# Stick-breaking attention: the scores copied to SBUF first, and the softplus and its running sum kept in one tile

## The chip, the cores and the metric

The kernel runs on one NeuronCore of a Trainium2 chip. The time is what the device took for one execution, in microseconds (us); lower is better. Five engines run side by side, each with its own queue of instructions, taken in order: TensorE (PE in the profile, with its weight loads as PEld), VectorE (DVE), ScalarE (ACT), GpSimd (POOL) and SyncE (SP), which here issues most transfers. They wait for one another through semaphores. Operands lie in SBUF; a matmul's results lie in PSUM, of which the stage below uses a pool of four banks.

## The reference

One decoder layer over 512 tokens of width 2048 in fp32: a norm, one input projection, two kinds of attention, an output projection, and an MLP of width 8192 with a squared ReLU. The change concerns the second kind, stick-breaking attention, with 16 heads of 64:

```python
z = jnp.einsum('bhqd,bhsd->bhqs', q_blk, kt).astype(jnp.float32) * scale
log_beta = jax.nn.log_sigmoid(z)
log_1m = jnp.where(causal, jax.nn.log_sigmoid(-z), 0.0)
later = lax.cumsum(log_1m, axis=3, reverse=True) - log_1m
w = jnp.where(causal, jnp.exp(log_beta + later), 0.0)
```

The weights w are then multiplied with v. With softplus(z) = max(z,0) + ln(1+exp(-|z|)), masked to the keys before the query, the exponent is z minus the sum of softplus from this key up to the query.

## The kernel before

Every large product is done as three matmuls of a high and a low half (`mm3`, lines 123 to 125). The halves of a weight chunk are made by ScalarE (a cast, line 91) and VectorE (a subtraction, line 92, 128x1024 here).

The stick-breaking heads go in eight pairs (0 to 7). A pair has four blocks of 128 queries (0 to 3); block i sees (i+1)*128 keys, so its tiles are 128 to 512 columns wide. In names such as z_30 and b_31 the first digit is the block and the second the head of the pair. A block has two halves. `begin` issues the score matmuls of both heads into two PSUM banks (line 558, six of them) and then, for each head, this chain:

- ScalarE: absolute value of the scores from PSUM (571), exp (572), ln (573), into tile a
- VectorE: max(z,0)+a into tile b, reading the scores from PSUM (574)
- GpSimd: mask of the diagonal 128x128 of b (575)
- VectorE: running sum of b into a (578), then z minus a into b, reading the scores from PSUM again (580)
- GpSimd: mask of b (581); ScalarE: exp of b, the weights (583)

`end` transposes the weights on TensorE (592, into a PSUM bank named wtr) and VectorE copies them to SBUF (593). After block 3 the pair's product with v follows (609, bank bv).

These blocks are interleaved with the projections' matmuls by `pump`, called after every 12 of them: on odd calls it runs the `begin` of the next block, and three calls after it, once a later block has begun, the matching `end`:

```python
if clock[0] % 2:
    begun = bool(units) and units[0][0] <= clock[0]
    if begun:
        begin, end = units.popleft()[1]
        begin()
        flight.append(end)
    flight.append(None) if not begun and flight else None
elif len(flight) > 1:
    end = flight.popleft()
```

So the transposes of a block stand in TensorE's queue 36 projection matmuls, and the `begin` of the next block, behind its scores. Within what the program says, a scheduler orders each engine's queue by its own estimates, and gives a PSUM bank of the pool of four (scores, wtr and bv together) to the next user of it; a bank is free once its last reader is done.

Of the kernel before, what the change touches and what calls it, by code (L numbers as in the profile page):

```python
# [15 lines left out]
ALU = mybir.AluOpType  # L16
# [4 lines left out]
P = 128  # L21
# [37 lines left out]
def hymba_layer(ctx: ExitStack, tc: tile.TileContext, x, norm_attn_g, w_in, q_norm_g, k_norm_g,  # L59
                sinks, rel_bias, swa_out_g, sb_out_g, w_out, norm_mlp_g, w_up, w_down, sel, eye, out):  # L60
    nc = tc.nc
    x, out = x[0], out[0]
# [23 lines left out]
    def bank(name):  # L86
        return pa.tile([P, 512], F32, tag="pa", name=name)
# [289 lines left out]
    def finish_o(av, branch, c, keep=False):  # L377

        if c == 0:
            nc.scalar.square(out=S[branch], in_=av)  # L380
        else:
            sq = wk.tile([P, T], F32, tag="we", name=f"osq{branch}_{c}")
            nc.scalar.square(out=sq, in_=av)
            nc.gpsimd.tensor_tensor(out=S[branch], in0=S[branch], in1=sq, op=ALU.add)
        if keep:
            return parts(av, branch, c)
        o = wk.tile([P, T], F32, tag="we", name=f"o{branch}_{c}")
        nc.scalar.copy(out=o, in_=av)
        nc.sync.dma_start(out=oscr[8 * branch + c], in_=o)
        return None  # L390
# [158 lines left out]
    def sb_pair(c, q, k, vs, keep):  # L549
        wt, ws_of = [], {}  # L550

        def scores(i):
            wn = max((i + 1) * P, 256)
            sc = [bank(f"z{c}_{i}{s}") for s in range(2)]
            for a, b in ((0, 0), (0, 1), (1, 0)):
                for s in range(2):
                    rows = slice(s * DH, (s + 1) * DH)
                    nc.tensor.matmul(sc[s][:, 0:wn], q[rows, a, i * P:(i + 1) * P], k[rows, b, 0:wn],
                                     start=(a == 0 and b == 0), stop=(a == 1))
            return sc  # L560

        def weights(i, sc):
            w = (i + 1) * P
            dg = slice(i * P, (i + 1) * P)
            ws = []
            for s in range(2):
                z = sc[s][:, 0:w]
                a = wk.tile([P, 512], F32, tag=("wa", "wc")[s], name=f"a{c}_{i}{s}")[:, 0:w]
                b = wk.tile([P, 512], F32, tag=("wb", "wd")[s], name=f"b{c}_{i}{s}")[:, 0:w]

                nc.scalar.activation(out=a, in_=z, func=AF.Abs)
                nc.scalar.activation(out=a, in_=a, func=AF.Exp, scale=-1.0)
                nc.scalar.activation(out=a, in_=a, func=AF.Ln, bias=1.0)
                nc.vector.scalar_tensor_tensor(out=b, in0=z, scalar=0.0, in1=a, op0=ALU.max, op1=ALU.add)
                nc.gpsimd.affine_select(out=b[:, dg], in_=b[:, dg], pattern=[[-1, P]], compare_op=ALU.is_gt,
                                        fill=0.0, base=0, channel_multiplier=1)

                nc.vector.tensor_tensor_scan(out=a[:, ::-1], data0=ones2[:, 0:1].broadcast_to([P, w]),
                                             data1=b[:, ::-1], initial=0.0, op0=ALU.mult, op1=ALU.add)
                nc.vector.tensor_tensor(out=b, in0=z, in1=a, op=ALU.subtract)  # L580
                nc.gpsimd.affine_select(out=b[:, dg], in_=b[:, dg], pattern=[[-1, P]], compare_op=ALU.is_gt,
                                        fill=NEG, base=0, channel_multiplier=1)
                nc.scalar.activation(out=b, in_=b, func=AF.Exp)
                ws.append(b)
            return ws

        def turn(i, ws):
            w = (i + 1) * P
            for s in range(2):
                tr = bank(f"wtr{c}_{i}{s}")  # L590
                for j in range(i + 1):
                    nc.tensor.transpose(tr[:, j * P:(j + 1) * P], ws[s][:, j * P:(j + 1) * P], ident)
                nc.vector.tensor_copy(out=wt[s][:, 0:i + 1, i * P:w],
                                      in_=tr[:, 0:w].rearrange("p (j q) -> p j q", q=P))

        def begin(i):
            ws_of[i] = weights(i, scores(i))

        def end(i):
            if i == 0:  # L600
                wt.extend(wtp.tile([P, 4, 512], F32, tag="wt", name=f"wt{c}_{s}") for s in range(2))
            turn(i, ws_of.pop(i))
            if i < 3:
                return
            av = bank(f"bv{c}")
            cc = c % 4
            for j in range(4):
                for s in range(2):
                    nc.tensor.matmul(av[s * DH:(s + 1) * DH, j * P:],
                                     vs[j][:, (2 * cc + s) * DH:(2 * cc + s + 1) * DH],  # L610
                                     wt[s][:, j, j * P:], start=(j == 0), stop=(j == 3))
            o = finish_o(av, 1, c, keep)
            if o is not None:
                ohl[1, c] = o

        return [(partial(begin, i), partial(end, i)) for i in range(4)]
# [445 lines left out]
    for cj in range(2 * NC):  # L1062
# [8 lines left out]
        for s, (name, ai, _, b, more) in enumerate(d_products(cj)):  # L1071
# [36 lines left out]
            a = act[c, ai]  # L1108
# [45 lines left out]
```

## Time and profile before

| | us |
|---|---|
| median of three runs | 1998.21 (1998.0 to 1998.86) |
| the profiled execution | 1998.97 |
| its span, first to last instruction | 1997.2 |
| TensorE busy | 1976.4 (99%) |
| VectorE busy | 1649.4 (83%) |
| ScalarE busy | 1037.5 (52%) |
| GpSimd busy | 1011.3 (51%) |

The stick-breaking blocks run from 320 to 626 us of the span. A timeline row gives the start, the duration, the engine and line, the tiles written and read with their sizes, how many instructions are merged into the row, and in brackets how long the engine stood idle before it and which instruction ended that. A merged row "x2" of 1.09 us holds two overlapping instructions. The granted clock (PEclk) is TensorE's, 1.00 at 2.4 GHz.

### The profile page before, as it was taken

Reading aid. Unit: us, or ns where it says so; the run is one execution under the profiler, and the core shown is the slowest. Engines: PE = TensorE matmul, PEld = TensorE weight load, DVE = VectorE, ACT = ScalarE, POOL = GpSimd, SP = SyncE. Lnnn points to the kernel's source line nnn. Section 1 sums busy time; section 2 is a strip of 40 time slices with the busy share of each in tenths; the row PEclk is TensorE's granted clock in tenths of the full one; section 3 lists DMA queues with packets and bytes.
Section 4 is the critical chain, followed back from the end, with each engine's and each line's share of the span. In section 5 each row is a group of like instructions: output and inputs, shape, how many; then the busy total and the mean of one; then the engine's idle time right before and its main releaser. Section 6 shows DMA issues by size and latency. Waiting matters only on the chain.

```text
span 1997.2 us, 31358 instructions
## 1 busy us (share of the span) xinstructions
PE 1976.4 (99%) x11652; PEld 1717.5 (86%) x11652; DVE 1649.4 (83%) x2142; ACT 1037.5 (52%) x1900; POOL 1011.3 (51%) x898
## 2 busy tenths in 40 slices
PE   8999999999999999999999999999999999999999
PEld 7887787778777889999999999998888888888887
DVE  4469654664776479999999999999999999999997
ACT  6357544453554575656565656565443333333444
POOL 0013431221321038777777777776866656656653
PEclk9999999999999999999999999999999999999999
DMA  6732332224245555665656565656766457456451
GB/s 224 146 119 80 100 98 83 75 69 137 93 140 172 192 169 180 217 201 189 208 181 215 180 216 181 212 176 245 290 250 250 158 221 291 161 221 261 143 204 67
DMA packets 213916, 350.31 MB, mean 175 GB/s; under 512 B 9779, under 2 KB 154372, under 8 KB 206596
## 3 DMA queue, kind: packets, MB, share of 16 engines
q1 hardware_dynamic: 211216, 345.02, 51.0%
q10 hardware_dynamic: 2548, 3.30, 1.3%
q8 instruction: 91, 1.49, 0.3%
q14 instruction: 61, 0.50, 0.1%
HBM read 270.16 MB, written 78.12 MB: 174 GB/s over the span
## 4 chain that ended last, share of the span: by engine, by line
PE 89%; DVE 5%; ACT 3%; POOL 1%; issue 1%; DMA 1%; POOLq 0%; SPq 0%; DVEq 0%; ACTq 0%
PE ps_u L831 11%; PE ps_u L830 11%; PE ps_u L832 11%; PE ps_d L1119 9%; PE ps_d L1120 9%; PE ps_d L1118 9%; PE ps_qk L123 3%; PE ps_qk L125 3%; PE ps_qk L124 3%; PE ps_o L125 2%; PE ps_o L123 2%; PE ps_o L124 2%; PE ps_qa L123 1%; PE ps_qa L124 1%; PE ps_qa L125 1%; DVE lo_d L92 1%
## 5 line engine op out<-in xcount | busy, mean ns | idle before, releaser
L832 PE MATMUL ps_u<-h2h,lo_u 128*128 128x256 f32 x1792 | 507.5, 283 | 0.1
L830 PE MATMUL ps_u<-h2h,hi_u 128*128 128x256 f32 x1792 | 507.6, 283 | 0.0
L831 PE MATMUL ps_u<-h2l,hi_u 128*128 128x256 f32 x1792 | 507.4, 283 | 0.0
L1118 PE MATMUL ps_d<-hi_d,ad 128*128 128x512 f32 x896 | 348.8, 389 | 2.7 <-ACT e L856 2.7
L1119 PE MATMUL ps_d<-lo_d,ad 128*128 128x512 f32 x896 | 349.0, 390 | 0.1
L1120 PE MATMUL ps_d<-hi_d,ad 128*128 128x512 f32 x896 | 348.7, 389 | 0.0
L832 PEld LDWEIGHTS ps_u<-h2h,lo_u 128*128 128x128 f32 x1792 | 344.1, 192 | 0.3 <-DVE lo_u L92 0.3
L831 PEld LDWEIGHTS ps_u<-h2l,hi_u 128*128 128x128 f32 x1792 | 344.2, 192 | 0.0
L830 PEld LDWEIGHTS ps_u<-h2h,hi_u 128*128 128x128 f32 x1792 | 344.1, 192 | 0.0
L806 POOL TENSOR_TENSOR s_u<-st_u 128x256 f32<-128x256 f32 x256 | 212.1, 849 | 245.1 <-DVE lo_u L92 176.3
L965 POOL TENSOR_TENSOR T<-st_d,T 128x1024 f32<-128x1024 f32 x64 | 174.2, 2724 | 188.3 <-DVE lo_d L92 185.8
L92 DVE TENSOR_TENSOR lo_d<-T,hi_d 128x1024 fp32r<-128x1024 f32 x128 | 250.5, 1971 | 19.5 <-ACT hi_d L91 18.9
L92 DVE TENSOR_TENSOR lo_u<-s_u,hi_u 128x512 fp32r<-128x512 f32 x256 | 261.8, 1023 | 0.3 <-ACT hi_u L91 0.3
L91 ACT CAST hi_u<-st_u 128x384 fp32r<-128x384 f32 x256 | 131.2, 513 | 229.4 <-PE ps_u L831 224.1
L91 ACT CAST hi_d<-T 128x1024 fp32r<-128x1024 f32 x128 | 134.9, 1055 | 188.5 <-PE ps_d L1120 175.6
L92 DVE TENSOR_TENSOR lo_u<-st_u,hi_u 128x384 fp32r<-128x384 f32 x256 | 196.1, 766 | 30.4 <-ACT hi_u L91 29.5
L1118 PEld LDWEIGHTS ps_d<-hi_d,ad 128*128 128x128 f32 x896 | 168.2, 188 | 38.0 <-ACT e L856 3.1
L1119 PEld LDWEIGHTS ps_d<-lo_d,ad 128*128 128x128 f32 x896 | 168.2, 188 | 36.1 <-DVE lo_d L92 1.3
L1120 PEld LDWEIGHTS ps_d<-hi_d,ad 128*128 128x128 f32 x896 | 168.2, 188 | 34.8
L92 DVE TENSOR_TENSOR lo_d<-st_d,hi_d 128x1024 fp32r<-128x1024 f32 x96 | 189.7, 1988 | 9.1 <-ACT hi_d L91 9.0
L91 ACT CAST hi_d<-st_d 128x1024 fp32r<-128x1024 f32 x96 | 101.3, 1056 | 154.3 <-PE ps_d L1120 135.4
L91 ACT CAST hi_u<-s_u 128x512 fp32r<-128x512 f32 x256 | 158.5, 619 | 18.0 <-POOL s_u L806 18.0
(242 smaller groups left out, 3818.9 us busy)
## 6 DMA issues: line engine op xcount, KB each, us to landing
st_u<-in_w_up SPq DMA_DIRECT2D x128, 512.0 KB, 3.7
st_d<-in_w_down SPq DMA_DIRECT2D x64, 1024.0 KB, 8.3
ad<-ac SPq DMA_DIRECT2D x56, 1024.0 KB, 6.3
ac<-ah SPq DMA_DIRECT2D x32, 896.0 KB, 4.0
ac<-al SPq DMA_DIRECT2D x32, 896.0 KB, 5.8
st_qk<-in_w_in SPq DMA_DIRECT2D x64, 256.0 KB, 3.0
st_o<-in_w_out SPq DMA_DIRECT2D x32, 512.0 KB, 4.2
st_qa<-in_w_in SPq DMA_DIRECT2D x16, 512.0 KB, 4.0
```

Of the source, the lines that this page charges most:

```text
L91: cast = nc.scalar.copy(out=hi, in_=st)
L92: nc.vector.tensor_tensor(out=lo, in0=st, in1=hi.bitcast(F32), op=ALU.subtract)
L123: nc.tensor.matmul(ps, ah, bh, start=first, stop=False)
L124: nc.tensor.matmul(ps, ah, bl, start=False, stop=False)
L806: last_sum[0] = nc.gpsimd.tensor_tensor(out=o, in0=a, in1=b, op=op)
L830: nc.tensor.matmul(o, wh[:, a], hh[:, b], start=first, stop=False, skip_group_check=True)
L831: nc.tensor.matmul(o, wh[:, a], hl[:, b], start=False, stop=False, skip_group_check=True)
L832: nc.tensor.matmul(o, wl[:, a], hh[:, b], start=False, stop=(k == KP - 1), skip_group_check=True)
L965: nc.gpsimd.tensor_tensor(out=o, in0=raw[cj, a, h], in1=raw[cj, b, h], op=ALU.subtract)
L1118: nc.tensor.matmul(o, al, bh[:, kk], start=first, stop=False, skip_group_check=True)
L1119: nc.tensor.matmul(o, al, bl[:, kk], start=False, stop=False, skip_group_check=True)
L1120: nc.tensor.matmul(o, ar, bh[:, kk], start=False, stop=end, skip_group_check=True)
```

## The change

ScalarE first copies the scores of a head from PSUM into b. The sum max(z,0)+a is written over a (it still reads the scores from PSUM), the mask and the running sum work in place on a, and the last subtraction takes b minus a, both in SBUF, in place over b. Tiles, shapes and every other instruction stay. 64 copies are added, one for each head of each block.

```diff
@@ -567,17 +567,18 @@
                 z = sc[s][:, 0:w]
                 a = wk.tile([P, 512], F32, tag=("wa", "wc")[s], name=f"a{c}_{i}{s}")[:, 0:w]
                 b = wk.tile([P, 512], F32, tag=("wb", "wd")[s], name=f"b{c}_{i}{s}")[:, 0:w]
+                nc.scalar.copy(out=b, in_=z)

                 nc.scalar.activation(out=a, in_=z, func=AF.Abs)
                 nc.scalar.activation(out=a, in_=a, func=AF.Exp, scale=-1.0)
                 nc.scalar.activation(out=a, in_=a, func=AF.Ln, bias=1.0)
-                nc.vector.scalar_tensor_tensor(out=b, in0=z, scalar=0.0, in1=a, op0=ALU.max, op1=ALU.add)
-                nc.gpsimd.affine_select(out=b[:, dg], in_=b[:, dg], pattern=[[-1, P]], compare_op=ALU.is_gt,
+                nc.vector.scalar_tensor_tensor(out=a, in0=z, scalar=0.0, in1=a, op0=ALU.max, op1=ALU.add)
+                nc.gpsimd.affine_select(out=a[:, dg], in_=a[:, dg], pattern=[[-1, P]], compare_op=ALU.is_gt,
                                         fill=0.0, base=0, channel_multiplier=1)

                 nc.vector.tensor_tensor_scan(out=a[:, ::-1], data0=ones2[:, 0:1].broadcast_to([P, w]),
-                                             data1=b[:, ::-1], initial=0.0, op0=ALU.mult, op1=ALU.add)
-                nc.vector.tensor_tensor(out=b, in0=z, in1=a, op=ALU.subtract)
+                                             data1=a[:, ::-1], initial=0.0, op0=ALU.mult, op1=ALU.add)
+                nc.vector.tensor_tensor(out=b, in0=b, in1=a, op=ALU.subtract)
                 nc.gpsimd.affine_select(out=b[:, dg], in_=b[:, dg], pattern=[[-1, P]], compare_op=ALU.is_gt,
                                         fill=NEG, base=0, channel_multiplier=1)
                 nc.scalar.activation(out=b, in_=b, func=AF.Exp)
```

From line 570 on the changed kernel's line numbers are one higher than before: the copy is 570, absolute value 572, exp 573, ln 574, max-and-add 575, first mask 576, running sum 579, subtraction 581, second mask 582, the weights' exp 584, transpose 593, its copy 594.

The instructions are also ordered anew. ScalarE, block 3 of pair 1, before, from the last weights of block 2 (b_21) on; hi_qk is a cast for the projections:

```order
L583 ACTIVATE b_21_3616<-b_21_3616 128x384
L571 ACTIVATE a_30_3674<-z_30_3666 128x512
L571 ACTIVATE a_31_3687<-z_31_3667 128x512
L572 ACTIVATE a_30_3674<-a_30_3674 128x512
L572 ACTIVATE a_31_3687<-a_31_3687 128x512
L573 ACTIVATE a_30_3674<-a_30_3674 128x512
L573 ACTIVATE a_31_3687<-a_31_3687 128x512
L91 CAST hi_qk_0_3972<-st_qk_0_3969 128x1024
L583 ACTIVATE b_30_3675<-b_30_3675 128x512
L571 ACTIVATE a_00_3748<-z_00_3740 128x128
L583 ACTIVATE b_31_3688<-b_31_3688 128x512
```

And the same place after the change:

```order
L584 ACTIVATE b_21_3629<-b_21_3629 128x384
L570 COPY b_30_3689<-z_30_3680 128x512
L572 ACTIVATE a_30_3688<-z_30_3680 128x512
L570 COPY b_31_3703<-z_31_3681 128x512
L573 ACTIVATE a_30_3688<-a_30_3688 128x512
L572 ACTIVATE a_31_3702<-z_31_3681 128x512
L574 ACTIVATE a_30_3688<-a_30_3688 128x512
L573 ACTIVATE a_31_3702<-a_31_3702 128x512
L91 CAST hi_qk_0_3994<-st_qk_0_3991 128x1024
L574 ACTIVATE a_31_3702<-a_31_3702 128x512
L584 ACTIVATE b_30_3689<-b_30_3689 128x512
```

Each head now has four instructions ahead of its sum instead of three, the two heads are staggered, and the cast hi_qk stands ahead of the second head's last logarithm. The exps of block 2 stand ahead of block 3's copy as they stood ahead of its absolute value.

VectorE, the same block, before (wt<-wtr are copies of transposes, lo_qk is a subtraction for the projections; the running sum is listed as SCALAR_TENSOR_TENSOR with the tile of ones):

```order
L574 SCALAR_TENSOR_TENSOR b_30_3675<-z_30_3666,a_30_3674 128x512
L574 SCALAR_TENSOR_TENSOR b_31_3688<-z_31_3667,a_31_3687 128x512
L578 SCALAR_TENSOR_TENSOR a_30_3674<-ones_494,b_30_3675 128x512
L578 SCALAR_TENSOR_TENSOR a_31_3687<-ones_494,b_31_3688 128x512
L580 TENSOR_TENSOR b_30_3675<-z_30_3666,a_30_3674 128x512
L580 TENSOR_TENSOR b_31_3688<-z_31_3667,a_31_3687 128x512
L593 COPY wt_0_3568<-wtr_20_3712 128x3x128
L593 COPY wt_1_3569<-wtr_21_3717 128x3x128
L92 TENSOR_TENSOR lo_qk_0_3973<-st_qk_0_3969,hi_qk_0_3972 128x1024
```

And after:

```order
L575 SCALAR_TENSOR_TENSOR a_30_3688<-z_30_3680,a_30_3688 128x512
L594 COPY wt_0_3580<-wtr_20_3728 128x3x128
L579 SCALAR_TENSOR_TENSOR a_30_3688<-ones_494,a_30_3688 128x512
L594 COPY wt_1_3581<-wtr_21_3733 128x3x128
L581 TENSOR_TENSOR b_30_3689<-b_30_3689,a_30_3688 128x512
L575 SCALAR_TENSOR_TENSOR a_31_3702<-z_31_3681,a_31_3702 128x512
L92 TENSOR_TENSOR lo_qk_0_3995<-st_qk_0_3991,hi_qk_0_3994 128x1024
L579 SCALAR_TENSOR_TENSOR a_31_3702<-ones_494,a_31_3702 128x512
L575 SCALAR_TENSOR_TENSOR a_00_3764<-z_00_3756,a_00_3764 128x128
L581 TENSOR_TENSOR b_31_3703<-b_31_3703,a_31_3702 128x512
```

Before, the two heads go side by side and the projections' subtraction comes behind both. Now the first head's chain is finished first, and lo_qk, and the first sum of the next pair's block 0, stand between the steps of the second head.

TensorE, the transposes of block 3 of pair 0 with what they wait for, before:

```order
L592 MATMUL wtr_30_3479<-ident,b_30_3368 128x128 [waits Activation_49]
L592 MATMUL wtr_30_3479<-ident,b_30_3368 128x128 x2
L592 MATMUL wtr_30_3479<-ident,b_30_3368 128x128 [waits Pool_49]
L592 MATMUL wtr_31_3485<-ident,b_31_3381 128x128 [waits Activation_49]
L592 MATMUL wtr_31_3485<-ident,b_31_3381 128x128 x2
L592 MATMUL wtr_31_3485<-ident,b_31_3381 128x128 [waits Pool_49]
```

And after:

```order
L593 MATMUL wtr_30_3489<-ident,b_30_3374 128x128 [waits Activation_49]
L593 MATMUL wtr_30_3489<-ident,b_30_3374 128x128 x2
L593 MATMUL wtr_30_3489<-ident,b_30_3374 128x128 [waits Pool_49]
L123 MATMUL ps_v_3343<-hi_v_2_3516,hT_238 128x512
L124 MATMUL ps_v_3343<-lo_v_2_3517,hT_238 128x512
L125 MATMUL ps_v_3343<-hi_v_2_3516,hT_238 128x512
L123 MATMUL ps_v_3343<-hi_v_2_3516,hT_246 128x512
L124 MATMUL ps_v_3343<-lo_v_2_3517,hT_246 128x512
L125 MATMUL ps_v_3343<-hi_v_2_3516,hT_246 128x512
L593 MATMUL wtr_31_3495<-ident,b_31_3388 128x128 [waits Activation_49]
L593 MATMUL wtr_31_3495<-ident,b_31_3388 128x128 x2
L593 MATMUL wtr_31_3495<-ident,b_31_3388 128x128 [waits Pool_49]
```

The second head's transposes (wtr_31) now come six projection matmuls behind the first head's. The same holds in pairs 3, 4 and 7; in pairs 1, 2, 5 and 6 they stay side by side.

## Rows read from the trace of the kernel before

**Rows 1.** the page, busy time by engine (microseconds, share of the span, instructions)

```profile
PE 1976.4 (99%) x11652; PEld 1717.5 (86%) x11652; DVE 1649.4 (83%) x2142; ACT 1037.5 (52%) x1900; POOL 1011.3 (51%) x898
```

**Rows 2.** waits, 320 to 626 us: engine, line, releaser, total us, times, longest

```profile
DVE b L574 <- ACT a L573: 61.5, 22, 6.0
ACT b L583 <- POOL b L581: 52.9, 28, 3.7
...
PEld z L558 <- DVE b L580: 9.8, 18, 1.1
```

**Rows 3.** windows: engines' busy us, granted clock (1.00 is full), DMA share, GB/s

```profile
core 0: us, PE busy (x) PEld busy (x) DVE busy (x) ACT busy (x) POOL busy (x), PEclk, DMA share, GB/s
343.00:346.00 3.00, 3.00 (x8) 2.20 (x8) 0.96 (x2) 3.00 (x7) 1.28 (x1) 0.56 0.32 59
514.00:517.00 3.00, 1.68 (x9) 0.77 (x7) 3.00 (x7) 0.52 (x1) 1.32 (x3) 1.00 0.00 0
320.00:626.00 306.00, 299.27 (x1449) 226.98 (x1448) 204.95 (x337) 162.74 (x342) 76.95 (x146) 0.99 0.34 105
```

**Rows 4.** timeline, TensorE, pair 1 into 2: start, duration, row, idle before, releaser

```profile
362.18 0.62 PE L558 MATMUL z<-hl_b,hl_b 64*128 64x256 f32 x6
...
376.55 0.50 PE L123 MATMUL ps_v<-hi_v,hT 128*128 128x512 f32 x1
...
382.58 0.39 PE L125 MATMUL ps_v<-hi_v,hT 128*128 128x512 f32 x1
383.61 1.21 PE L558 MATMUL z<-hl_b,hl_b 64*128 64x256 f32 x6 [0.64 <-DVE b L580]
...
387.61 1.04 PE L592 MATMUL wtr<-ident,b 128*128 128x128 f32 x8
```

**Rows 5.** timeline, ScalarE, the same stretch

```profile
375.60 0.99 ACT L583 ACTIVATE b<-b 128x384 f32<-128x384 f32 x2 [2.09 <-POOL b L581]
376.54 1.09 ACT L571 ACTIVATE a<-z 128x512 f32<-128x512 f32 x2
...
384.70 0.62 ACT L583 ACTIVATE b<-b 128x512 f32<-128x512 f32 x1
```

**Rows 6.** timeline, VectorE, the same stretch

```profile
379.21 1.29 DVE L574 SCALAR_TENSOR_TENSOR b<-z,a 128x512 f32<-128x512 f32 x2 [1.80 <-ACT a L573]
380.42 2.56 DVE L578 TENSOR_TENSOR_SCAN a<-ones,b 128x512 f32<-128x512 f32 x2
382.89 1.26 DVE L580 TENSOR_TENSOR b<-z,a 128x512 f32<-128x512 f32 x2
...
385.00 1.21 DVE L92 TENSOR_TENSOR lo_qk<-st_qk,hi_qk 128x1024 fp32r<-128x1024 f32 x1
```

**Rows 7.** timeline, GpSimd, the masks of pairs 0 and 1

```profile
351.16 1.22 POOL L575 TENSOR_SCALAR_AFFINE_SELECT b<-b 128x128 f32<-128x128 f32 x1 [0.24 <-DVE b L574]
...
380.63 1.09 POOL L575 TENSOR_SCALAR_AFFINE_SELECT b<-b 128x128 f32<-128x128 f32 x1 [0.30 <-DVE b L574]
...
384.28 0.29 POOL L581 TENSOR_SCALAR_AFFINE_SELECT b<-b 128x128 f32<-128x128 f32 x1 [0.30 <-DVE b L580]
```

**Rows 8.** groups by shape, 320 to 626 us: count, busy us, mean ns, idle

```profile
L578 DVE TENSOR_TENSOR_SCAN a<-ones,b 128x512 f32<-128x512 f32 x16 | 19.5, 1219 | 1.1 <-POOL b L575 0.4
...
L580 DVE TENSOR_TENSOR b<-z,a 128x512 f32<-128x512 f32 x16 | 10.3, 674 | 0.0
...
L388 ACT COPY o<-bv 128x512 f32<-128x512 f32 x6 | 3.5, 581 | 0.0
```

**Rows 9.** timeline, TensorE, last block of pair 0

```profile
340.68 0.50 PE L558 MATMUL z<-hl_b,hl_b 64*128 64x512 f32 x1 [0.66 <-DVE b L580]
341.94 1.40 PE L558 MATMUL z<-hl_b,hl_b 64*128 64x512 f32 x5 [0.77 <-DVE wt L593]
...
355.56 0.66 PE L592 MATMUL wtr<-ident,b 128*128 128x128 f32 x4 [0.80 <-ACT b L583]
```

**Rows 10.** timeline, TensorE, last block of pair 3

```profile
440.00 1.06 PE L558 MATMUL z<-hl_b,hl_b 64*128 64x512 f32 x6
...
450.01 1.03 PE L592 MATMUL wtr<-ident,b 128*128 128x128 f32 x8
```


## The prediction

> **What bounds the kernel now.** I read the busy times first: TensorE is busy for 99% of the span [rows 1], so only time in which TensorE stands still, or runs at a lower clock, can be gained or lost. Next the windows: the change touches 320 to 626 us, where TensorE is idle for 306.00 - 299.27 = 6.7 us, and some more is lost inside its busy time by a slow clock and by matmuls that start late [rows 3]. Then the waits of that stretch: the release that TensorE's score matmuls wait for is VectorE's subtraction b (line 580), the last reader of the scores, 18 times and 9.8 us on the weight loads [rows 2]. Last the timeline of one place that repeats. When pair 1 ends and pair 2 begins, the scores of pair 2's block 0 start at 383.61, 1.03 us after the projection matmul before them (382.58), where 0.23 is the rhythm: 0.8 lost; and their six matmuls take 1.21 us where the same block shape takes 0.62 without a wait: 0.59 lost [rows 4]. That 1.39 us is there at the end of four pairs (1, 2, 5, 6). Pair 0 loses more: its block 3 scores wait 0.66 and 0.77, its second transposes 0.80 [rows 9], and the clock falls to 0.56 right after [rows 3]. In pair 4 the same two score waits stand within 514 to 517, TensorE 1.68 of 3.00 busy, at a clock of 1.00 [rows 3].
>
> So what ends last is the chain of a block: scores, three ScalarE steps, sum, mask, running sum, subtraction, mask, exp. It holds the scores' banks until the subtraction, and it must end before TensorE wants the weights.
>
> **The change part by part.**
>
> *The earlier release.* The scores' last reader moves from the subtraction (580) to the max-and-add, two VectorE steps sooner. Absolute value and max-and-add still read PSUM, so the copy by itself frees nothing. In pair 1 the banks of pair 2's block 0 then hang on pair 1's first sum and on a copy of block 2's transposes, both due by 383, so the 1.39 us goes: -1.4 in each of four pairs, -5.6. In pair 0 the score waits go too.
>
> *The copies.* No copy of scores is in the trace. The nearest row is ScalarE's copy of a 128x512 PSUM tile, 0.581 us [rows 8]; two absolute values of that size take 1.09, so one more costs about 0.5 of queue [rows 5]. ScalarE is half idle [rows 1], so the two copies cost nothing in throughput; they cost in the chain. By the order, the first head's ln is ScalarE's sixth instruction of the block, not its fifth: +0.5; the second's is eighth behind a cast.
>
> *The subtraction.* From PSUM it takes 0.674 for 512 columns [rows 8]. With both operands in SBUF the nearest row is the projections' subtraction, 1.21 for 1024 [rows 6], so 0.6: no gain worth counting. The Trainium skill, "VectorE: DVE Perf Modes", section "Rules for kernel authors", advises a copy out of PSUM where many operations follow; the rows show 0.674 against 0.6 for the one operation that follows here, so by that page too the sum stays.
>
> *The masks.* A mask of 128x128 on GpSimd takes 0.29 [rows 7]. But it took 1.09 at 380.63, beside the running sum that began at 380.42 [rows 6, 7], and 1.22 at 351.16. It took 0.29 at 384.28 beside the subtraction and copies, which read PSUM [rows 6, 7]. The mask thus waits out a VectorE instruction that began earlier and reads two SBUF tiles. After the change the second mask of the second head comes right behind a subtraction whose follower on VectorE is, in block 2 of pairs 1 and 2, the projections' subtraction (1.21), and in block 3 the next pair's running sum: up to 1.21 - 0.29 = 0.9, and nothing at the least. I take the whole of it, as the row at 351.16 is the same pairing. The Trainium skill, "SBUF — State Buffer", section "Who interferes with whom", says that a VectorE instruction with two SBUF inputs contends with a GpSimd one that reads SBUF, and that the one issued later is blocked; the trace agrees (1.09 against 0.29).
>
> *The new order, pair 1, block 3.* Before: block 2's second exp ends at 376.59, block 3's first sum starts at 379.21 and its second exp ends at 384.70 + 0.62 = 385.32 [rows 5, 6]. The second transposes are wanted half of 1.04 behind the first ones' 387.61 [rows 4], about 388.1, and 386.65 if the 1.39 is gone. After:
> - Block 2: its sum is some 0.35 later by the copies, the two copies of block 1's transposes now stand among its steps (+0.7), and its last mask is locked (+0.9). Its second exp ends at 378.6, not 376.59. It stands ahead of block 3's first copy on ScalarE, so block 3, whose scores are there at 376.55, starts 2.0 late.
> - ScalarE: five instructions of 0.5 and an ln of 0.63 from 378.5: first sum at 381.7.
> - VectorE, in its new order: sum 381.7, copy, running sum 382.85, copy, subtraction 384.45, second head's sum 385.05, projections' subtraction 385.65 to 386.87. That locks the second head's first mask, so its running sum (1.22, rows 8) starts at 387.05; the subtraction starts at 388.43, its mask is locked by the next pair's running sum until 389.5, and the exp ends at 390.1.
> TensorE wants it at 386.65: a wait of 3.45, for 1.39 lost before; with a little on the product with v, +2.3. Without the lock in block 2, as in pairs 5 and 6 where a copy stands between, some 0.65 less. Bounds: with block 2 in time (-2.0) and no lock on the last mask (-0.5) the exp ends at 387.6, a wait of 1.0, net -0.4; with every estimate 1 us late, +3.3.
>
> *Sum.* Pairs 1 and 2: 2 x 2.3. Pairs 5 and 6: 2 x (2.8 - 1.4). Pair 3 loses no time before; its transposes start at 450.01; the second head's, 0.4 behind, move by six matmuls more, so they are wanted at 451.8. Its scores are there at 440.00 + 1.06 = 441.06 [rows 10]; pair 1's chain takes 390.1 - 378.5 = 11.6 from block 2's last exp, which stands here one place later, behind the first absolute value, and costs 0.6: 453.3, so +1.5. Pair 7, the same but with less behind it: +0.2, an estimate. Pair 0 loses its two score waits as starts show them (1.9), the transposes' 0.97 (0.80 of idle and a late start) and the slow clock, (1 - 0.56) x 3.0 = 1.3; it takes a wait like pair 3's: 1.5 - 4.2 = -2.7. Pair 4 gives 3.00 - 1.68 = 1.3 and takes 1.5: +0.2. Together 4.6 + 2.8 + 1.5 + 0.2 - 2.7 + 0.2 = +6.6. Clock: it fell once after waits of 1.4 us and once it did not [rows 3]; of four waits of about 3 us I let two bring a fall at 1.3 each: +2.6. That is +9.2 on the profiled 1998.97, or on the median 1998.21: 2007.4, told as 2007.
>
> **The rivals.**
> - *An even trade.* The scheduled order is not what the engines' own pace gives. If block 2's exp is not late, the new waits are 1.0 to 2 us and eat what the early release gives: between -4 and +4, middle 1998. For it: slack of 1.3 us at block 3 and about 3 us at block 2 in the trace before; against it: the second head's steps stand behind lo_qk by order, not by estimate.
> - *Faster.* One mechanism: the banks. If the last exp of block 3 ends by 386.65 in pair 1's time, no wait comes in place of the released ones. Then 5.6 in four pairs, 4.2 less little in pair 0, and 1.3 in pair 4 go: about -10, 1988. It is decided at the second exp of block 3: 385.32 before, so it may be 1.3 later. For it: every wait of the score matmuls was on the subtraction. Against it: the copies, the order and the locks all push that exp later, 4.8 by the sum above.
> - *Much slower.* The forecast's waits with the clock falling after each of six: 6.6 + 6 x 1.3 = +14.4, 2012; with every chain 1 us later in the six pairs another 6, 2018.
> - *The change does nothing for the banks,* because another reader is last: then the 5.6 and pair 0's 1.9 stay and the chains are late in addition; but the waits for scores delay the wants too, so this is within the forecast's price.
>
> **How the numbers follow.** Forecast 0.55, much slower 0.08, even trade 0.25, faster 0.12. A difference under 0.2% (4 us) can't be told from none here. Faster than 1994: 0.12, from the faster rival. Within 4 us: 0.25. Slower than 2002: 0.63. The range goes from 1995, which takes in nearly all of the even trade, to 2017, short of the last of the much slower case; the forecast's own range is 2003 to 2014.
>
> **What would show it.** After the change no score matmul of a next pair's block 0 waits on VectorE's subtraction; TensorE waits instead on ScalarE's exp at the second transposes of block 3, 3 us or so in pairs 1 and 2, less in 5 and 6, 1 to 2 in pair 3. The masks' mean (second one, 0.3 before) rises. Block 2's second exp ends after block 3's scores are there. VectorE's busy time stays, ScalarE's rises by 64 copies of 0.26 to 0.58. In pair 0 the clock does not fall at 343; it falls after some of the new waits. Wrong if the second transposes hardly wait, or if the waits for scores stay.

## The result and the profile after

The changed kernel takes 2021.53 us (median of four runs, 2020.07 to 2021.87), the kernel before 1998.53 in the same measurement: ratio 1.0115, 95% interval 1.01 to 1.0131. It is slower by 23 us. The forecast was 2007, with a range up to 2017: the direction holds, the size is wrong by more than a factor of two. The profiled execution took 2021.24, its span is 2019.4.

The waits of 320 to 650 us (columns as in [rows 2]; the columns of the others are as in the groups ahead):

```profile
PEld wtr L593 <- ACT b L584: 25.0, 18, 3.5
...
PEld z L558 <- DVE a L575: 1.7, 3, 0.8
...
PEld z L558 <- DVE b L581: 1.1, 3, 0.4
```

The score matmuls hardly wait on the subtraction any more: three times, 1.1 us in all on the weight loads, where [rows 2] had 18 times and 9.8 us. TensorE waits on ScalarE's exp at the transposes instead. The timeline of TensorE, at the last transposes of block 2 in pair 0, and at the end of pairs 1, 3 and 7:

```profile
345.69 0.55 PE L593 MATMUL wtr<-ident,b 128*128 128x128 f32 x3 [0.86 <-ACT b L584]
...
382.56 1.09 PE L558 MATMUL z<-hl_b,hl_b 64*128 64x256 f32 x6 [0.27 <-DVE a L575]
...
386.45 0.61 PE L593 MATMUL wtr<-ident,b 128*128 128x128 f32 x4
390.33 1.11 PE L593 MATMUL wtr<-ident,b 128*128 128x128 f32 x4 [3.27 <-ACT b L584]
...
462.87 0.66 PE L593 MATMUL wtr<-ident,b 128*128 128x128 f32 x4 [2.06 <-ACT b L584]
...
643.46 0.66 PE L593 MATMUL wtr<-ident,b 128*128 128x128 f32 x4 [0.60 <-ACT b L584]
...
646.71 0.66 PE L593 MATMUL wtr<-ident,b 128*128 128x128 f32 x4 [1.21 <-ACT b L584]
```

In pair 1, answering to [rows 4], the first transposes at 386.45 hardly wait, and the second ones come at 390.33, 3.3 us idle. The forecast had the want at 386.65 and the exp's end at 390.1. How the exp gets there, on ScalarE, answering to [rows 5]:

```profile
378.27 0.52 ACT L584 ACTIVATE b<-b 128x384 f32<-128x384 f32 x1 [2.35 <-POOL b L582]
378.70 0.57 ACT L570 COPY b<-z 128x512 f32<-128x512 f32 x1
...
389.64 0.63 ACT L584 ACTIVATE b<-b 128x512 f32<-128x512 f32 x1 [1.69 <-POOL b L582]
```

Block 2's second exp ends at 378.79, not 376.59; the copy starts block 3 at 378.70, and the second exp ends at 390.27. On VectorE, answering to [rows 6] (the last three rows are pair 7):

```profile
381.81 0.69 DVE L575 SCALAR_TENSOR_TENSOR a<-z,a 128x512 f32<-128x512 f32 x1 [3.73 <-ACT a L574]
...
385.75 1.22 DVE L92 TENSOR_TENSOR lo_qk<-st_qk,hi_qk 128x1024 fp32r<-128x1024 f32 x1
387.15 1.23 DVE L579 TENSOR_TENSOR_SCAN a<-ones,a 128x512 f32<-128x512 f32 x1 [0.19 <-POOL a L576]
...
388.48 0.68 DVE L581 TENSOR_TENSOR b<-b,a 128x512 f32<-128x512 f32 x1
...
642.49 1.33 DVE L579 TENSOR_TENSOR_SCAN a<-ones,a 128x512 f32<-128x512 f32 x1 [0.19 <-POOL a L576]
643.75 1.19 DVE L92 TENSOR_TENSOR lo_o<-st_o,hi_o 128x1024 fp32r<-128x1024 f32 x1
644.86 0.68 DVE L581 TENSOR_TENSOR b<-b,a 128x512 f32<-128x512 f32 x1
```

The first sum is at 381.81 (forecast 381.7), the projections' subtraction at 385.75 (385.65), the second running sum at 387.15 (387.05), the second subtraction at 388.48 (388.43). GpSimd's masks, answering to [rows 7]:

```profile
377.07 1.16 POOL L582 TENSOR_SCALAR_AFFINE_SELECT b<-b 128x128 f32<-128x128 f32 x1 [1.72 <-DVE b L581]
...
385.90 1.22 POOL L576 TENSOR_SCALAR_AFFINE_SELECT a<-a 128x128 f32<-128x128 f32 x1 [0.22 <-DVE a L575]
388.69 0.62 POOL L576 TENSOR_SCALAR_AFFINE_SELECT a<-a 128x128 f32<-128x128 f32 x1 [1.57 <-DVE a L575]
389.31 0.29 POOL L582 TENSOR_SCALAR_AFFINE_SELECT b<-b 128x128 f32<-128x128 f32 x1
```

The second mask of block 2's second head is held by a projections' subtraction (1.16 instead of 0.29), the first mask of block 3's second head too (1.22). The last one (389.31) is not held itself, but stands behind another that is (388.69, 0.62). Over the stage the second masks take 0.380 us on average, 0.312 before. The clock, answering to [rows 3], fell in three places of the stage (to 0.50, which is 1.2 GHz), and no longer in pair 0:

```profile
core 0: us, PE busy (x) PEld busy (x) DVE busy (x) ACT busy (x) POOL busy (x), PEclk, DMA share, GB/s
389.00:396.00 7.00, 5.67 (x18) 3.84 (x20) 4.08 (x9) 2.09 (x4) 1.44 (x5) 0.53 0.33 107
577.00:581.00 4.00, 4.00 (x14) 2.11 (x14) 2.85 (x5) 1.06 (x3) 0.35 (x2) 0.57 0.04 3
611.00:615.00 4.00, 3.27 (x10) 2.07 (x12) 3.67 (x8) 2.09 (x4) 0.84 (x4) 0.57 0.13 50
```

And two groups by shape: the copy costs 0.577 and the subtraction from SBUF 0.681, as good as the 0.581 and 0.674 of [rows 8]:

```profile
L581 DVE TENSOR_TENSOR b<-b,a 128x512 f32<-128x512 f32 x16 | 10.9, 681 | 0.0
...
L570 ACT COPY b<-z 128x512 f32<-128x512 f32 x16 | 9.2, 577 | 0.2 <-PE z L558 0.2
```

What each pair cost, worked out from TensorE's timeline: the time from the first score matmul of a pair's block 1 to that of the next pair (pair 0 from its own first score matmul, pair 7 to a projection matmul behind its product, the same one in both: 633.07 before, 653.99 after).

| pair | before | after | difference | forecast |
|---|---|---|---|---|
| 0 | 41.89 | 41.30 | -0.6 | -2.7 |
| 1 | 32.20 | 37.52 | +5.3 | +2.3 |
| 2 | 32.24 | 36.23 | +4.0 | +2.3 |
| 3 | 74.45 | 77.80 | +3.3 | +1.5 |
| 4 | 34.26 | 34.97 | +0.7 | +0.2 |
| 5 | 32.81 | 36.36 | +3.5 | +1.4 |
| 6 | 32.25 | 34.58 | +2.3 | +1.4 |
| 7 | 32.67 | 34.98 | +2.3 | +0.2 |
| sum | | | +21.0 | +6.6, and 2.6 of clock without a pair |

The whole span grew by 22.2 us, so 1.2 us more came behind the stage. There, at the start of the down projection, the clock fell once more, as it did not before (columns as in the windows above):

```profile
1410.00:1414.00 4.00, 4.00 (x11) 3.23 (x12) 4.00 (x5) 3.75 (x7) 3.12 (x1) 0.58 1.02 430
```

### The profile page after: what moved, and what is told of

Read it like the earlier page. It is cut to its first block, busy times and chain, and to the rows that moved or that the text cites. A ratio compares the mean times of both kernels' runs of the same rounds, so it can differ in the third digit from the quotient of the medians.

```text
span 2019.4 us, 31424 instructions
## 1 busy us (share of the span) xinstructions
PE 1983.0 (98%) x11652; PEld 1717.2 (85%) x11652; DVE 1651.9 (82%) x2142; ACT 1060.3 (53%) x1964; POOL 1012.2 (50%) x898
## 4 chain that ended last, share of the span: by engine, by line
PE 84%; DVE 6%; ACT 4%; POOL 2%; issue 2%; DMA 2%; POOLq 0%; SPq 0%; DVEq 0%; ACTq 0%
PE ps_u L832 10%; PE ps_u L831 10%; PE ps_u L833 10%; PE ps_d L1119 10%; PE ps_d L1120 10%; PE ps_d L1121 10%; PE ps_qk L123 2%; PE ps_qk L125 2%; PE ps_qk L124 2%; DVE a L579 2%; PE ps_o L125 2%; PE ps_o L123 2%; PE ps_o L124 2%; PE ps_qa L123 1%; PE ps_qa L124 1%
```

## The experiments

Times are medians beside the kernel before on the same chip, with the ratio and its interval.

**steps.** The change written step by step for both heads, instead of head by head; the same instructions.

```diff
-            for s in range(2):
-                ...copy, Abs, Exp, Ln, max-and-add, mask, running sum, subtract, mask, Exp of head s
+            for s in range(2):
+                nc.scalar.copy(out=B_[s], in_=z[s])
+            for s in range(2):
+                nc.scalar.activation(out=A_[s], in_=z[s], func=AF.Abs)
+            ...and so on, a loop over the heads for each step
```

> The change with the same instructions, but written step by step for both heads instead of head by head, so that on VectorE the two heads go side by side again and the projections' subtraction comes behind both. Theory A (the loss is the order that the copies bring about: the projections' subtraction and the next pair's first steps inside the second head's chain): the second transposes of block 3 hardly wait any more, 1990 to 1998 us. Theory B (the loss is the added copies on ScalarE and the masks locked by the subtraction from SBUF, whatever the order): 2012 us or more, with waits of 2 us or more left at the transposes.

Measured: 2012.79, ratio 1.0072 (1.0057 to 1.0087). The time is at the foot of theory B's range, the waits are between the two: writing it step by step takes back some 10 of the 23 us, not all. In pair 0 a wait of 2.95 us is left at the transposes, in pairs 1, 2, 5 and 6 at most 0.9. In pair 1 it falls from 3.3 us to 0.41, but the product with v now waits 1.74:

```profile
388.71 1.34 PE L599 MATMUL wtr<-ident,b 128*128 128x128 f32 x8 [0.41 <-ACT b L590]
...
392.72 2.96 PE L616 MATMUL bv<-wt,v 128*64 128x512 f32 x16 [1.74 <-DVE wt L600]
```

On VectorE the copies of those transposes (392.0) stand behind the next pair's block 0, and that stands behind the late exps on ScalarE:

```profile
391.60 0.46 DVE L585 TENSOR_TENSOR b<-b,a 128x128 f32<-128x128 f32 x2
391.99 1.27 DVE L600 COPY wt<-wtr 128x512 f32<-128x512 f32 x2
```

**before_steps.** The kernel before, no copy, written step by step in the same way (the sum and its mask in b, the subtraction from the scores).

> The kernel before, no copy, written step by step for both heads; VectorE's order is then the same as in steps, side by side in all eight pairs (before, it is so in six). If the writing itself is free: 1994 to 2000 us (pairs 0 and 4 may gain the wait of their second transposes, 1 us), so that the copies' own price at this order is steps less this run, 12 us or more. If the writing costs: 2004 us or more, and steps says less of the copies.

Measured: 2002.56, ratio 1.0014 (1.0005 to 1.0024), between the two ranges. The writing itself costs about 3 us, so at this order the copies with what hangs on them cost 10: steps less before_steps, each against its own baseline.

**inplace_only.** The change without its copy.

```diff
-                nc.scalar.copy(out=b, in_=z)
-                nc.vector.tensor_tensor(out=b, in0=b, in1=a, op=ALU.subtract)
+                nc.vector.tensor_tensor(out=b, in0=z, in1=a, op=ALU.subtract)
```

> The change without the copy: max-and-add, mask and running sum in place on a, the subtraction from PSUM into b. VectorE's order is that of before. Theory A and theory B: 1998 us within 2. If reading and writing one tile in place slows VectorE or the masks: over 2002 us and a longer running sum than 1.22 us.

Measured: 1999.27, ratio 1.0002 (0.9993 to 1.0012). Working in place is free; everything lost hangs on the copy and on the subtraction that reads it.

**copy_only.** The kernel before with the copy added.

```diff
+                nc.scalar.copy(out=b, in_=z)
                 nc.scalar.activation(out=a, in_=z, func=AF.Abs)
```

> The kernel before with the copy alone (what it writes is overwritten later), sums and subtraction as before, from PSUM. VectorE's order is nearly that of the change. Theory A: slow like the change, 2012 to 2030 us; as the scores' banks are again held until the subtraction, waits of score matmuls of block 0 stand beside those of the transposes. Theory B (the locks by the subtraction from SBUF matter most): those are gone, so at most 2010 us.

Measured: 2016.84, ratio 1.0091 (1.0075 to 1.0106). Theory A's range: 17 of the 23 us come with the copy alone. Theory B had the held masks gone here; they are not. The subtraction reads PSUM, yet the second masks take 0.491 us on average (0.380 in the change); VectorE's order in pair 1 is that of the change, and a projections' subtraction follows block 2's chain as it does there. What the other 6 us are was not tried. Waits of the scores stand beside those of the transposes, mostly through banks that the copies of transposes free:

```profile
PE wtr L593 <- ACT b L584: 8.2, 7, 2.1
...
PE z L558 <- DVE wt L594: 4.4, 8, 1.3
```

**late_steps.** steps with the copies behind the logarithms.

```diff
-            for s in range(2):
-                nc.scalar.copy(out=B_[s], in_=z[s])
             ...
                 nc.scalar.activation(out=A_[s], in_=A_[s], func=AF.Ln, bias=1.0)
+            for s in range(2):
+                nc.scalar.copy(out=B_[s], in_=z[s])
```

> The step by step form (steps) with the two copies of a block behind its two logarithms on ScalarE instead of ahead of the absolute values; everything else as in steps, VectorE's order too. Theory C (what is left in steps, 13 us over before, is in two parts: the copies' 1.0 us in each block's ScalarE chain, which delays the exp of block 2 and the sum of block 3; and VectorE's copies of the last transposes, which now come behind the next pair's block 0, so that the product with v waits): the first part goes, no waits at the transposes in pairs 1, 2, 5 and 6, the waits at the product with v stay: 1996 to 2006 us. Rival D (the place of the copy does not matter, as ScalarE must do it anyway before it gets to the next block): 2010 us or more.

Measured: 2012.32, ratio 1.0068 (1.0053 to 1.0083): no gain over steps, a miss of theory C and in rival D's range. The reason is in the waits. The max-and-add needs nothing of the copy, yet in late_steps it waits for it; in steps it waited for the logarithm (first late_steps, then steps):

```profile
DVE a L577 <- ACT b L575: 68.1, 30, 5.9
```

```profile
DVE a L577 <- ACT a L575: 68.7, 29, 6.6
```

ScalarE's logarithms and copies, and VectorE's sum, in late_steps:

```profile
379.51 1.15 ACT L573 ACTIVATE a<-a 128x512 f32<-128x512 f32 x2
380.55 1.07 ACT L575 COPY b<-z 128x512 f32<-128x512 f32 x2
```

```profile
381.16 1.29 DVE L577 SCALAR_TENSOR_TENSOR a<-z,a 128x512 f32<-128x512 f32 x2 [0.68 <-ACT b L575]
```

The first logarithm ends at 379.51 + 0.6, the first copy at 380.55 + 0.6, and the sum starts at 381.16. Both read the same PSUM bank, and of two such reads the one written later waits: in copy_behind_sum, below, where the sum is written first, it is the copy that waits for the sum:

```profile
ACT b L575 <- DVE a L574: 5.6, 20, 0.9
```

The Trainium skill, "PSUM — Partial Sum Buffer", section "PSUM bank collisions raise a hardware error ⚠️", says that two engines may not access the same partitions of one bank at once, reads included, and that the compiler's scheduler adds a dependency between such instructions; the trace agrees (sum and end of the copy within 0.1 us).

**late_heads.** The change, head by head, with the copy written behind the logarithm.

```diff
-                nc.scalar.copy(out=b, in_=z)
                 ...
                 nc.scalar.activation(out=a, in_=a, func=AF.Ln, bias=1.0)
+                nc.scalar.copy(out=b, in_=z)
```

> The change, head by head as it stands, with the copy moved behind the logarithm in the program. On VectorE the projections' subtraction then comes behind block 3 in pairs 1, 2, 3, 5 and 6, and inside its chain in pairs 0 and 4 as before the change. Theory A and C: between late_steps and the change, nearer late_steps, 1998 to 2009 us, with the transposes waiting mainly in pairs 0 and 4. Rival D: 2012 us or more.

Measured: 2020.55, ratio 1.0112 (1.0097 to 1.0127): a miss, in rival D's range. The scheduler placed the copies ahead of the logarithms all the same (in block 3 of pair 1 behind the first head's absolute value, 377.57, and the second head's exp, 380.09), so the chain was not relieved.

**copy_behind_sum.** The change with the copy one step later still.

```diff
-                nc.scalar.copy(out=b, in_=z)
                 ...
                 nc.vector.scalar_tensor_tensor(out=a, in0=z, scalar=0.0, in1=a, op0=ALU.max, op1=ALU.add)
+                nc.scalar.copy(out=b, in_=z)
```

> The change with its copy moved by one thing only: behind the max-and-add, so that on ScalarE it no longer stands between the scores and the first sum; the banks are then released by the copy. VectorE's order becomes that of the kernel before. Theory E (the copy costs by its place: the max-and-add reads the same PSUM bank and is held until the copies written ahead of it are done, in late_steps by 0.5 us behind the copy; the waits at the product with v in steps follow from the same lateness, as the next pair's block 0 stands behind the late exp on ScalarE): waits at transposes and products of 1 us or more go in pairs 1, 2, 3, 5, 6 and 7, block 0's scores hardly wait: 1990 to 2001 us. Rival F (the early release itself costs, as the next pair's block 0 crowds VectorE before the copies of the last transposes): product waits stay near 2 us in pairs 1, 2, 5 and 6: 2003 us or more.

Measured: 2007.05 (2003.64 to 2007.47), ratio 1.004 (1.0025 to 1.0055). Moving one line takes back 14 of the 23 us: the copy costs by its place, and with its place goes VectorE's order, which in pair 1 is that of the kernel before again; the two are not separated here. But theory E's 1990 to 2001 is missed, and rival F's sign is there. TensorE, end of pair 1:

```profile
383.42 0.62 PE L558 MATMUL z<-hl_b,hl_b 64*128 64x256 f32 x6
...
386.87 1.03 PE L593 MATMUL wtr<-ident,b 128*128 128x128 f32 x8
...
389.79 2.87 PE L610 MATMUL bv<-wt,v 128*64 128x512 f32 x16 [1.42 <-DVE wt L594]
```

The scores of block 0 (383.42, 0.62 long) wait for nothing, and the transposes hardly. The product waits 1.42 us, as much as the scores waited before (1.39). VectorE says why:

```profile
388.57 0.47 DVE L581 TENSOR_TENSOR b<-b,a 128x128 f32<-128x128 f32 x2
388.96 1.28 DVE L594 COPY wt<-wtr 128x512 f32<-128x512 f32 x2
```

The copies of the transposes stand behind block 0's chain, which starts after ScalarE's exps whatever the banks do. Pairs 1 and 2 take 32.33 and 32.37 us, against 32.20 and 32.24 before: in these pairs the early release brings nothing. Nor do they lose anything. Of the 3.7 us that the eight pairs lose in this trace, pairs 0 and 4 lose 2.2. The traced execution is the fastest of the four (2003.64), so 3.4 of the median's 9 us are not in the trace.

**before_later_begin** and **copy_behind_sum_later_begin.** The kernel before, and copy_behind_sum, with block 0 of a pair begun one pump later, behind the old pair's last transposes:

```diff
-                begin()
+                if flight and begin.args[0] == 0 and 'sb_pair' in begin.func.__qualname__:
+                    held.append(begin)
+                else:
+                    begin()
...
             end()
+            if held:
+                held.pop()()
```

> The kernel before, no copy, but a pair's block 0 begins one pump later, right behind the last transposes of the pair before it (12 projection matmuls later on TensorE). Theory G (the 1.4 us wait of block 0's scores and the wait of the product with v are one thing: the next pair's block 0 begins before the old pair's chain is done, and whichever of the two is freed, the other waits): neither waits now, at no cost, as block 0 has 8 us to spare: 5 us or so less than before, 1990 to 1996 us. If the score waits have to be paid elsewhere (transposes or banks): 1997 us or more.

Measured: 1998.76, ratio 0.9996 (0.9987 to 1.0004): no change, a miss; the score waits moved to block 3, in pairs 1 to 3, 5 and 7.

> copy_behind_sum with the same later begin of block 0. Theory G: the product's waits of 1.4 us in pairs 1, 2, 5 and 6 go, 5 to 7 us less than copy_behind_sum, and the early release brings nothing beyond before_later_begin: within 4 us of it or slower. If the early release were worth something once the order allows it: 3 us or more faster than before_later_begin.

Measured: 2001.69, ratio 1.001 (1.0001 to 1.0019): 7 us less than copy_behind_sum, each against its own baseline (+2.2 and +9.4), as theory G has it, and not faster than before_later_begin. In pairs 1, 2, 5 and 6 no product waits any more.

**all_three.** Step by step, the copy behind the max-and-add, block 0 later.

> Step by step, the copy behind the max-and-add, and block 0 of a pair begun one pump later. If the early release has worth once nothing stands against it: no waits of 1 us at scores, transposes of block 3 or products, 1989 to 1996 us, faster than the kernel before and than before_later_begin. If it has none: 1997 us or more.

Measured: 1999.19, ratio 0.9998 (0.9989 to 1.0008). In pair 1 neither scores nor transposes wait, and the product 0.18:

```profile
382.80 1.03 PE L604 MATMUL wtr<-ident,b 128*128 128x128 f32 x8
...
384.48 2.96 PE L621 MATMUL bv<-wt,v 128*64 128x512 f32 x16 [0.18 <-DVE wt L605]
387.38 0.62 PE L563 MATMUL z<-hl_b,hl_b 64*128 64x256 f32 x6
```

That pair takes 30.90 us, 1.3 less than before. But pairs 3, 4 and 7 are 4 us longer together, and the total is that of the kernel before, as expected of an early release without worth.

**steps_psub.** steps with the subtraction from PSUM.

> The step by step form (steps) with the subtraction from PSUM, as before the change; the copy stays first and is overwritten. It takes away the early release of the banks and the subtraction with two operands in SBUF, at nearly one order. Theory C: the waits of block 0's scores come back (2 us or more in pairs 1, 2, 5, 6) and those at the product with v go, so 2010 to 2022 us. If the locked masks are what is left in steps: under 2008 us, and second masks of 0.29 us.

Measured: 2009.98, ratio 1.0054 (1.0037 to 1.0071), at the edge of theory C's range. The product's waits go in pairs 1, 2, 5 and 6, as theory C has it, but the scores of block 0 wait only 0.37 there, not 2; block 3's scores wait 2.1 in pairs 0 and 4. The second masks, first in steps, then here:

```profile
L587 POOL TENSOR_SCALAR_AFFINE_SELECT b<-b 128x128 f32<-128x128 f32 x64 | 24.9, 400 | 45.5 <-DVE b L585 43.5 <-PE ps_qk L124 2.0
```

```profile
L587 POOL TENSOR_SCALAR_AFFINE_SELECT b<-b 128x128 f32<-128x128 f32 x64 | 19.6, 313 | 49.0 <-DVE b L585 46.3 <-PE z L558 1.2 <-PE wtr L599 0.9
```

0.400 against 0.313 on average: masks held by a subtraction with two SBUF operands are seen, and cost little here: against their own baselines the two runs are 2 us apart, within what they are good to.

**early_mask.** The change, with its second mask moved to the copy.

```diff
                 nc.scalar.copy(out=b, in_=z)
+                nc.gpsimd.affine_select(out=b[:, dg], in_=b[:, dg], ..., fill=NEG, ...)
                 ...
                 nc.vector.tensor_tensor(out=b, in0=b, in1=a, op=ALU.subtract)
-                nc.gpsimd.affine_select(out=b[:, dg], in_=b[:, dg], ..., fill=NEG, ...)
```

> The change with its second mask put on the copy of the scores right after the copy, instead of behind the subtraction (the fill is so large that the sums do not alter it). It takes the mask's hand-over, and its lock, out of the end of the chain; the order is otherwise nearly the change's. By the sum of the forecast the exp of block 3's second head is 1.5 us or so earlier in pairs 1 and 2 (0.9 from block 2, 0.5 from the last lock, and the mask's own 0.3 with its hand-over), and 0.8 elsewhere: 6 to 9 us less than the change, 2011 to 2016 us. If the locks cost nothing at the end that counts: 2018 us or more.

Measured: 2011.32, ratio 1.0064 (1.0049 to 1.0079), in the range: 10 us less than the change. The mask at the chain's end, with what holds it and its hand-over, is worth that. In pair 1 the second transposes wait 1.74, not 3.3:

```profile
387.84 0.66 PE L593 MATMUL wtr<-ident,b 128*128 128x128 f32 x4 [1.74 <-ACT b L584]
```

**one_mask** and **post_mask.** A single mask on the copy with all steps reading the copy; and step by step, the copy behind the max-and-add with the second mask on it at once.

> The copy, then one mask on it with the large negative fill, and everything behind it from the copy in SBUF (softplus of the fill is 0, its weight 0, so the other two masks go). The bank is free after the copy; in the steady pairs VectorE's order is side by side. Theory A: 1988 to 1998 us, no waits of 1 us at block 3's transposes in pairs 1, 2, 5 and 6. Theory B: the copies stay, so 2005 us or more.

Measured: 2014.11, ratio 1.0077 (1.0062 to 1.0092). Theory A is missed, theory B's range holds. In pairs 1, 2, 5 and 6 the transposes do not wait, as expected, but the products do (1.6 to 2.2 us), here at the end of pair 5:

```profile
568.86 3.92 PE L608 MATMUL bv<-wt,v 128*64 128x512 f32 x11 [2.16 <-DVE wt L592]
```

> The step by step form with the copy behind the max-and-add and the second mask put on the copy at once, so that the exp follows the subtraction directly. Theory E: the chain is shorter than before by a mask and its hand-over (0.3 to 0.5 us) and the banks are free before they are wanted: 1986 to 1997 us, faster than the kernel before. Rival F: 2000 us or more.

Measured: 2009.64, ratio 1.0051 (1.0034 to 1.0068), a miss of theory E and in rival F's range: the product waits in pairs 1, 2, 5 and 6 (1.8 in pair 1).

No version beats the kernel before clearly.

## Why the prediction was wrong

Right: what bounds the kernel, the early end of the score waits, the copy as a cost of the chain and not of throughput, the price of copy and subtraction, the lateness of block 2's exp, the masks that are held, and the order with lo_qk inside the second head's chain. For pair 1 the working met the trace within 0.2 us at every step on VectorE and at the last exp. In pairs 5 and 6 the idle gap before the second transposes is 2.6 us, 2.8 in the sum.

Part of that closeness is luck. Pair 1 began 0.6 us earlier on TensorE than before (its block 1 scores at 361.56, not 362.18), which the forecast's absolute times left out. Measured from its own scores, block 2's second exp is 2.8 us later than before, not 2.0: block 1's second exp is late too (369.31), and block 2's first copy stands behind it (369.63). And the running sum of the next pair, which was to hold the last mask until 389.5, did not: the mask ended at 389.6 because it stood behind another that was held.

Wrong was the sum over the other places, all in one direction. Of 22.2 us in the span 9.2 were forecast; 13 are missing:
- *Pairs 0, 3, 4 and 7.* The forecast gave them -2.7 + 1.5 + 0.2 + 0.2 = -0.8; they cost -0.6 + 3.3 + 0.7 + 2.3 = +5.7. That is 6.5 of the 13 us missing, and the step that failed. In pair 3 the second transposes wait 2.06 (462.87), where no wait stood before and 1.5 was forecast. Pair 3's figure was carried from pair 1's chain, pair 7's 0.2 was an estimate without an order read. On VectorE in pair 7 lo_o stands between the second head's running sum and its subtraction (642.49, 643.75, 644.86), and both transposes wait (0.60 and 1.21). In pair 0 the gains were counted, but block 2's own second transposes (345.69, 0.86 idle), which waited nowhere before, were not looked at.
- *The clock.* Two falls at 1.3 us were added. There were three in the stage, and the longest lasted 7 us: estimated as (1 - clock) times TensorE's busy time, 5.67 x 0.47 + 4.00 x 0.43 + 3.27 x 0.43 = 5.8 us. Against the 2.6 forecast that is 3.2 more. The fourth, behind the stage, was not in the sum at all: 4.00 x 0.42 = 1.7 us by the same estimate, about the 1.2 us that the span lost there.
- *The rest of pairs 1, 2, 5 and 6.* Their forecast with the clock was 4.6 + 2.8 + 2.6 = 10.0; measured 15.1. Beside the clock's 3.2 there remain 1.9 us. In pair 1 the scores of block 0 still took 1.09 us (0.27 idle on the first sum) where the whole 1.39 was counted as gone: the sum that frees the bank was late by then itself. The same in pair 2 (1.08, 0.39 idle), which had no fall of the clock and still cost 4.0 instead of 2.3.

The much slower rival came nearest. Its clock term, 6 x 1.3 = 7.8 us, is about what the clock cost (5.8 + 1.7), by fewer and longer falls; with every chain 1 us later it reached 2018, still short of the 2021.53. The even trade fell at its condition: block 2's exp was late.

The faster rival failed for a reason that the forecast did not have. It said that if the last exp came in time, the released waits would be a gain. In copy_behind_sum the exp does come in time in pairs 1, 2, 5 and 6, and the gain is still not there, since the product with v takes the same 1.4 us. The scores' wait was not caused by the bank alone: the next pair's block 0 begins before the old pair's chain is through, and holds VectorE against it. With block 0 begun later the product's waits go (copy_behind_sum_later_begin, all_three).

How the 23 us divide, from differences of runs on their own baselines, each good to 2 us or so: written step by step, the copies with what hangs on them cost about 10 (steps less before_steps). Written head by head, they cost 23. The other 12 or 13 come only with the head-by-head form, and the order that the copies bring about there is what differs in the traces; that the two parts simply add was not shown. The direct difference, the change less steps, is 10, as steps also pays the 3 us of its own writing. The copies' part is a matter of place: behind the max-and-add the change loses 9 instead of 23. Why the scheduler orders the heads so once a copy stands ahead was not tried. What takes the gain of the steady pairs back in all_three was seen (pairs 3, 4 and 7), not experimented on; in before_later_begin, which has no copy, pairs 3 and 7 are 0.9 us longer each, so part of it comes with the later begin.

## What to carry to other kernels

A copy on a half idle engine is not free if it stands in a chain whose end another engine waits for: count it in the chain, and once more for every block whose tail it delays. Before crediting a wait that goes, look for what would wait next at the same place, and read the order at every place where the pattern differs, not at the one that is easiest to compute. Where two engines read the same PSUM bank, the order in which the reads are written was a wait here too (late_steps, copy_behind_sum).

## What the runs showed of the hardware

The clock is not a function of the wait alone. At the start of the down projection TensorE waits before the change and after it. Before, timeline and the window behind the wait:

```profile
1388.36 0.47 PE L1118 MATMUL ps_d<-hi_d,ad 128*128 128x512 f32 x1 [2.72 <-ACT e L856]
```

```profile
1388.00:1392.00 4.00, 3.64 (x16) 3.07 (x17) 4.00 (x5) 4.00 (x8) 3.54 (x2) 1.00 1.01 428
```

And in copy_behind_sum, timeline and the window behind it:

```profile
1392.26 0.47 PE L1119 MATMUL ps_d<-hi_d,ad 128*128 128x512 f32 x1 [2.83 <-DMA ad<-ac]
```

```profile
1394.00:1398.00 4.00, 4.00 (x13) 3.17 (x12) 4.00 (x5) 3.12 (x7) 1.38 (x1) 0.66 1.02 424
```

The wait is 2.7 us there and 2.8 here; the clock stays at 1.00 there and falls here, to a mean of 0.66 over 4 us. In the changed kernel the same wait of 2.75 us (to 1409.97) was followed by the fall to 0.58 shown above. Part of the spread between runs of one kernel goes with the clock: the four runs of steps took 2014.68 and 2014.86 at a mean granted clock of 0.996 and 0.997, 2010.89 and 2010.81 at 0.998 and 0.999. Why the clock falls in one run and not in the other is not shown.
